# Gate vectors taken as columns, parted weights in two rings, and the pooling sums by a scan

## The chip, the cores and the metric

The kernel runs on one core of a Trainium2 chip. The metric is the device time of one execution in microseconds (us). Engines are named as in the profile: PE is TensorE's matmul side and PEld its weight load, DVE is VectorE, ACT is ScalarE, POOL is GpSimd, SP is SyncE, whose queue (SPq) issues nearly all DMAs here.

## The reference

Two layers of a decoder trunk on 1024 tokens of width 1024, in float32. Each layer has a mixing and a feed-forward sub-layer; both are normalised before and after and modulated by vectors that come from a conditioning vector `c`:

```python
c_act = silu(c)
for l in range(2):
    mod = c_act @ ada_w[l] + ada_b[l]          # 6 vectors of 1024
    shift_m, scale_m, gate_m, shift_f, scale_f, gate_f = split(mod, 6)

    h = rms_norm(x, g_pre_mix[l]) * (1.0 + scale_m) + shift_m
    q, k, v, u = split(h @ w_in[l] + b_in[l], [512, 640, 768])
    q, k = partial_rotary(q), partial_rotary(k)
    attn_out = sliding_window_attention_with_sinks(q, k, v, sinks[l])   # 8 heads of 64, window 128
    pool_out = causal_pool_mixer(u, pool_w[l], pool_scale[l])
    mix = concatenate([attn_out, pool_out]) @ w_out[l]
    x = x + gate_m * rms_norm(mix, g_post_mix[l])

    h = rms_norm(x, g_pre_ffn[l]) * (1.0 + scale_f) + shift_f
    f = (silu(h @ w_gate[l]) * (h @ w_up[l])) @ w_down[l]               # width 2816
    x = x + gate_f * rms_norm(f, g_post_ffn[l])
```

The pooling mixer has four groups of 128 channels. Group g takes, for each token, the mean over the last w = 2, 4, 8 or 16 tokens (fewer at the start), less the token itself, and multiplies by a 128 x 128 matrix.

## The kernel before, in words

**Products.** A float32 product is made of three matmuls of a rounded part `hi` (copied by ACT, L223) and a rest `lo` (subtracted by DVE, L224): hi by hi, hi by lo, lo by hi (`mm3`). Nearly all PE matmuls have 128 x 128 weights and 512 columns. A `STEP` of the hand-written pace is twelve of them. The sequence is handled in two halves of 512 tokens (h = 0, 1) of four tiles of 128.

**Stages of a layer.** First the mixing sub-layer: the projections `u_pass`, `q_pass`, `kv_pass` of a half, with attention and pooling of a half woven between the matmuls, and the output projection `mix_out`. There the order on PE is written out (`manual_schedule`): `weave` takes matmuls of the dense stream and, whenever the count of issued columns has reached a side chain's due time, a step of that chain. A chain's step yields the number of STEPs until it is due again: `LEADS` for the six stages of an attention group (split keys and queries; transposes; first scores; second scores and softmax; probabilities; values), a literal for the pooling mixer, the flow of `ada` weights and the gates. A group is four query heads of one tile of 128 tokens; there are 32 in all. Outside the mixing the order is left to the scheduler, with `run` handing out steps of side streams in proportion to steps of a main stream: first the up projection (`up_pair`, eleven pairs), then the down projection (seven products, 77 steps). In the trace, layer 0's mixing lies at about 75 to 290 us, its up projection until 766, its down projection until about 960; layer 1's mixing at about 970 to 1215, its up projection until 1690, and then its down projection to the end.

**Weights.** `weight` loads 128 x 512 floats into `raw`, then splits them into tiles of the rings `hi` and `lo` (three tiles of 128 x 1024 each, handed out in halves by `part`). Weights that both halves use are written back to DRAM split, and read back for the second half by `weight_once` (L247) as one whole 128 x 1024 tile of the ring `lo`: 28 such loads. `one_ahead` asks for a weight one step before it is used, and in the last `u_pass` two steps. The attention takes halves of `hi` tiles for the split keys and queries.

**Modulation.** A block of 512 values of `mod` is made by DVE: `acc`, 128 x 512, sums eight weight tiles times a column of `c_act` (L368 in the streams, L581 in the flows; eight loads of 256 KB), and PE sums it over the partitions. For scales and shifts of the next layer's mixing `ada_columns` does this with `acc` as weights and a column of ones, four matmuls with one column each, which come out as columns (L512; each float32 matmul appears as two instructions). A gate is a row: `ada_gate` splits `acc` in `hi` and `lo`, multiplies each (L542, L543; 512 columns, one weight column), adds a row of `ada_b`, multiplies a row of the norm's weights and stores the row to DRAM; `load_gate` reads it back onto all partitions. The mixing gate of each layer is made in its own mixing (`gate_flow`), the feed-forward gate in the up projection (`side`), and the next layer's columns in the down projection.

**Pooling.** `pool_mix` makes the sum over w tokens by doubling: log2(w) additions of some 520 elements (L1152), then the mean less the token (L1156), a split, and the matmuls. The tile of `u` has the last 16 tokens of the half before ahead of its 512 tokens (zeros for h = 0).

**End.** In layer 1's last product (`p4`), each evicted block is square-summed by ACT (L614), multiplied by the gate in place (L1778), then scaled and added to the residual in `finish` (from L750), and stored.

## Time and profile before

| | |
|---|---|
| median of three runs | 1868.26 us (1867.52 to 1868.6) |
| profiled execution | 1870.79 us |
| its span | 1869.1 us |
| granted TensorE clock, mean | 0.997 |
| PE busy | 1835.1 us |
| DVE busy | 1501.5 us |
| ACT busy | 919.7 us |
| first PE instruction, last PE end | 11.8 us, 1860.5 us |

The span runs from the first to the last instruction of the profiled execution, whose own time has 1.7 us around it. In lists of waits, a row has the engine and what it made, then what it waited for, then the sum in us, the number of waits and the longest. In a timeline a row has the start, the duration, engine, line, operation, tiles and count, and in brackets the idle time before it with what ended it. In groups a row has the count, the busy us, the mean in ns and the idle time before.

### The profile page before, as it was taken

The numbers are of one execution on the slowest core, as the hardware profiler recorded it, in microseconds if no ns is written. First come the engines' busy times: TensorE is split into PE (matmuls) and PEld (weight loads), VectorE is DVE, ScalarE is ACT, GpSimd is POOL, SyncE is SP. The second block draws the span as 40 slices with busy tenths as digits, with TensorE's granted clock in tenths as the row PEclk, the third lists the DMA queues.
The fourth block names the chain that finished last, engine by engine and source line by source line (L and its number), as shares of the span: only waits on it lengthen the run. The fifth ranks groups of instructions, "written<-read, shape, count | busy, mean of one in ns | idle before, by whom it ended". The sixth has DMA issues, their size and how long they took to land.

```text
span 1869.1 us, 25361 instructions
## 1 busy us (share of the span) xinstructions
PE 1835.1 (98%) x8662; PEld 1515.4 (81%) x8662; DVE 1501.5 (80%) x2492; ACT 919.7 (49%) x1757; POOL 100.3 (5%) x204
## 2 busy tenths in 40 slices
PE   7999999999999999999999999999999999999998
PEld 5888888888888888888887788888887887888886
DVE  7899885688888978879778788856878888877687
ACT  4885785562222223445648559755522222244452
POOL 0021130000000000000001202200000000000000
PEclk9999999999999999999999999999999999999999
DMA  9646744665456556844586676446646456574343
GB/s 341 201 141 215 259 147 143 208 215 181 167 188 218 183 180 225 298 147 133 194 302 202 213 233 217 155 135 209 220 157 207 162 200 229 176 270 142 113 146 114
DMA packets 237089, 363.84 MB, mean 195 GB/s; under 512 B 17912, under 2 KB 126344, under 8 KB 236960
## 3 DMA queue, kind: packets, MB, share of 16 engines
q1 hardware_dynamic: 236352, 360.13, 57.2%
q10 hardware_dynamic: 576, 2.10, 0.3%
q8 instruction: 68, 1.11, 0.2%
q14 instruction: 61, 0.50, 0.1%
q0 software_dynamic: 32, 0.00, 0.0%
HBM read 274.59 MB, written 87.57 MB: 194 GB/s over the span
## 4 chain that ended last, share of the span: by engine, by line
PE 83%; DVE 8%; DMA 4%; ACT 3%; issue 1%; SPq 1%; DVEq 0%; POOL 0%; ACTq 0%; POOLq 0%
PE acc L285 75%; PE msc L285 3%; PE msc L290 2%; PE pv L285 2%; DVE lo L224 1%; DMA raw<-in_w_up_dram 1%; DMA raw<-in_w_in_dram 1%; ACT hi L223 1%; DVE fn L1322 1%; SPq L426 0%; DVE ada L581 0%; DMA ar<-x 0%; DVE st L1026 0%; ACT sb L1034 0%; DVE raw L1337 0%
## 5 line engine op out<-in xcount | busy, mean ns | idle before, releaser
L223 ACT ACTIVATE hi<-raw 128x1024 fp32r<-128x1024 f32 (+2 forms) x360 | 315.6, 889 | 385.2 <-PE acc L285 243.6
L224 DVE TENSOR_TENSOR lo<-raw,hi 128x1024 fp32r<-128x1024 f32 (+2 forms) x360 | 363.0, 1016 | 115.9 <-ACT hi L223 110.7
L285 PE MATMUL acc<-t,hi 128*128 128x512 f32 x1408 | 432.1, 390 | 3.2 <-ACT hi L223 3.2
L285 PEld LDWEIGHTS acc<-t,hi 128*128 128x128 f32 x1408 | 263.6, 188 | 59.7 <-ACT hi L223 5.6
L285 PE MATMUL acc<-t,lo 128*128 128x512 f32 x704 | 271.9, 389 | 0.8 <-DVE lo L224 0.8
L285 PE MATMUL acc<-hT,hi 128*128 128x512 f32 x832 | 260.2, 394 | 0.0
L285 PE MATMUL acc<-hT,lo 128*128 128x512 f32 x608 | 213.4, 393 | 0.5 <-DVE lo L224 0.4
L285 PE MATMUL acc<-bh,hi 128*128 128x512 f32 x520 | 202.8, 390 | 0.0
L285 PE MATMUL acc<-bh,lo 128*128 128x512 f32 x520 | 202.4, 389 | 0.0
L1322 DVE TENSOR_TENSOR fn<-acc,fn 128x512 f32<-128x512 f32 x220 | 150.8, 686 | 33.7 <-PE acc L285 33.6
L285 PEld LDWEIGHTS acc<-hT,hi 128*128 128x128 f32 x832 | 151.8, 188 | 28.1
L285 PEld LDWEIGHTS acc<-t,lo 128*128 128x128 f32 x704 | 132.1, 188 | 30.0 <-DVE lo L224 2.4
L285 PEld LDWEIGHTS acc<-hT,lo 128*128 128x128 f32 x608 | 112.4, 188 | 25.8 <-DVE lo L224 1.3
L285 PE MATMUL acc<-ph,hi 128*128 128x512 f32 x328 | 126.5, 390 | 0.0
L1247 ACT ACTIVATE fn<-fn 128x512 f32<-128x512 f32 x44 | 27.9, 633 | 188.2 <-DVE fn L1322 188.2
L285 PEld LDWEIGHTS acc<-bh,lo 128*128 128x128 f32 x520 | 97.6, 188 | 20.4
L285 PEld LDWEIGHTS acc<-bh,hi 128*128 128x128 f32 x520 | 97.6, 188 | 20.2
L285 PE MATMUL acc<-b,hi 128*128 128x512 f32 x352 | 108.4, 389 | 0.0
L285 PE MATMUL acc<-lo,hT 128*128 128x512 f32 (+1 forms) x352 | 95.8, 349 | 3.9 <-DMA lo<-parted 2.9
L223 ACT ACTIVATE bh<-two_b 128x512 fp32r<-128x512 f32 x100 | 62.3, 623 | 71.2 <-PE acc L285 70.5
L285 PE MATMUL acc<-hi,hT 128*128 128x512 f32 (+1 forms) x320 | 88.8, 351 | 0.6 <-ACT hT L223 0.5
L285 PE MATMUL acc<-hi 128*128 128x512 f32 x224 | 87.6, 391 | 0.8 <-DVE fn L806 0.8
(320 smaller groups left out, 3235.3 us busy)
## 6 DMA issues: line engine op xcount, KB each, us to landing
raw<-in_w_gate_dram SPq DMA_DIRECT2D x44, 512.0 KB
raw<-in_w_up_dram SPq DMA_DIRECT2D x44, 512.0 KB
cfb<-in_ada_w_dram SPq DMA_DIRECT2D x80, 256.0 KB
raw<-keeps SPq DMA_DIRECT2D x40, 512.0 KB
keeps<-fn SPq DMA_DIRECT2D x66, 256.0 KB
ar<-in_ada_w_dram SPq DMA_DIRECT2D x64, 256.0 KB
two_b<-in_w_down_dram SPq DMA_DIRECT2D x30, 512.0 KB
lo<-parted SPq DMA_DIRECT2D x28, 512.0 KB
```

Source lines behind the costliest of these rows:

```text
L223: a = nc.scalar.activation(hi, src, AF.Copy)
L224: v = nc.vector.tensor_sub(lo, src, hi.bitcast(F32))
L285: return nc.tensor.matmul(dst, lhs, rhs, start=start, stop=stop)
L290: return nc.tensor.transpose(dst, src, eye_)
L1247: nc.scalar.activation(g, g, AF.Silu)
L1322: nc.vector.tensor_add(halves_of(dst)[m], bank, halves_of(src)[m])
```

## The change

1. `weight_once` takes the tile for a parted weight from `hi` and `lo` in turn, not always from `lo`.
2. `ada_gate_columns` makes a gate as columns, as `ada_columns` does: four one-column matmuls for a half, the bias and the norm's weights from two more groups of rows in `load_col_rows` (two loads more), and after the second half one transpose, a copy and a store of the row. It is used for both feed-forward gates and for layer 1's mixing gate, which is made in layer 0's down projection; `gate_flow` returns at once in layer 1. Layer 0's mixing gate is made as before.
3. `ada_stream` no longer closes a block at once: the close is appended to `pending`, and `settle`, called at each step of the main stream, carries it out.
4. The scores' scale moves into the copy of the queries; the negative maximum comes from the reduction itself; the sinks are no longer scaled.
5. For w = 8 and 16 `pool_mix` makes the sums by one scan over the tokens, token t in and token t - w out; in the second half it starts from a sum over the w tokens before.
6. In layer 1's last two products the multiplication by the gate writes to a tile of its own (`ready`).
7. Numbers of the pace change: `CLOSE`, `GAPS`, `LEADS`, some gaps, and the down projection's side stream gets 42 steps, not 28.

The diff, cut to its core:

```diff
     def weight_once(key, *srcs):
         if key in parted:
-            both = part("lo", 1024)
+            recent["ring"] = "hi" if recent.get("ring") == "lo" else "lo"
+            both = part(recent["ring"], 1024)
             nc.sync.dma_start(both.bitcast(F32), parted.pop(key))
...
-    NROW = 6 * KD + 2 * KD + 4 + 4
+    NROW = 6 * KD + 4 * KD + 4 + 4
...
-            (pool_scale[l], 4), (b_in[l, QKV:INW], 4),
+            (pool_scale[l], 4), (b_in[l, QKV:INW], 4), (g_post_mix[l], KD), (g_post_ffn[l], KD),
...
+    def ada_gate_columns(l, sub, cols):
+        gates[l, sub] = row = dr.tile([1, D], F32, tag="gate", name="gate", bufs=2 * DEPTH)
+        gc = t_("colp", [P, KD])
+        def close(half, acc):
+            bank = msc_bank()
+            for i in range(4):
+                nc.tensor.matmul(
+                    bank[:, i : i + 1], acc[:, i * P : (i + 1) * P], ones[:, 0:1], start=True, stop=True
+                )
+            o = slice(half * 4, half * 4 + 4)
+            b0 = (3 * sub + 2) * KD
+            g0 = 8 * KD + 8 + sub * KD
+            nc.vector.tensor_add(gc[:, o], bank[:, 0:4], cols[:, b0 + o.start : b0 + o.stop])
+            nc.vector.tensor_mul(gc[:, o], gc[:, o], cols[:, g0 + o.start : g0 + o.stop])
+            if half:
+                pending.append([1, turned])
+        def turned():
+            bank = msc_bank()
+            nc.tensor.transpose(bank[0:KD, :P], gc, ident)
+            rows = t_("ar", [P, 512])[:KD, :P]
+            nc.scalar.activation(rows, bank[0:KD, :P], AF.Copy)
+            nc.sync.dma_start(row.rearrange("o (k p) -> (o k) p", p=P), rows)
...
-    CLOSE = 1.89
-    GAPS = (0.71, 1.06)
+    CLOSE = 1.51
+    GAPS = (0.89, 1.06)
...
+    def settle(steps=1):
+        while due := [p for p in pending if p[0] <= steps]:
+            for p in due:
+                pending.remove(p)
+                p[1](*p[2:])
+            if steps < DONE:
+                break
+        for p in pending:
+            p[0] -= steps
     def ada_stream(jobs):
         for l, n0, close, *whole in jobs:
             got = []
             yield from ada_sum(l, n0, got, *whole)
-            yield from close(*got) or ()
+            pending.append([1, close, *got])
...
-        nc.scalar.activation(qT, bank, AF.Copy)
+        nc.scalar.activation(qT, bank, AF.Copy, scale=SCALE)
...
-        nc.vector.tensor_reduce(mx, S, axis=mybir.AxisListType.X, op=ALU.max)
-        nc.vector.tensor_scalar(mx, mx, -SCALE, None, op0=ALU.mult)
+        nc.vector.tensor_reduce(mx, S, axis=mybir.AxisListType.X, op=ALU.max, negate=True)
...
-    LEADS = (0.9, 0.85, 0.21, 2.72, 1.2, 0.94)
+    LEADS = (0.85, 0.9, 0.25, 2.45, 1.27, 1.0)
...
+            if w >= 8:
+                begin = 0.0
+                if h:
+                    begin = t_("st", [P, 8])[:, 0:1]
+                    nc.vector.tensor_reduce(
+                        begin, u[:, HALO - w : HALO], axis=mybir.AxisListType.X, op=ALU.add
+                    )
+                cur, width = t_("pt", [P, UW])[:, : HALO + T], w
+                nc.vector.tensor_tensor_scan(
+                    cur[:, HALO:n], u[:, HALO:n], u[:, HALO - w : n - w], begin, ALU.add, ALU.subtract
+                )
             while width < w:
...
         def gate_flow():
+            if l:
+                return
...
-            jobs = ada_columns(l + 1, 0, nxt["cols"], nxt["abm"])
-        side = ada_stream(ada_gate(l, 1))
+            jobs = ada_columns(l + 1, 0, nxt["cols"], nxt["abm"]) + ada_gate_columns(l + 1, 0, nxt["cols"])
+        side = ada_stream(ada_gate_columns(l, 1, par["cols"]))
...
-                    nc.vector.tensor_mul(fn[1][t][:, 0:512], fn[1][t][:, 0:512], G[:, 0:512])
-                    finish(1, t, fn[1], ss[1], G, tail[t], aheads[t])
+                    nc.vector.tensor_mul(ready[t][:, 0:512], fn[1][t][:, 0:512], G[:, 0:512])
+                    finish(1, t, ready, ss[1], G, tail[t], aheads[t])
...
-            (between(), 7 * NPAIR), (side, 28),
+            (between(), 7 * NPAIR), (side, 42),
```

More of the change, by code (lines that the diff above doesn't have):

```diff
@@ L551, in ada_gate @@
         ]
+    def ada_gate_columns(l, sub, cols):
[20 more added lines that the diff above has]
+            nc.sync.dma_start(row.rearrange("o (k p) -> (o k) p", p=P), rows)
+        return [
+            (l, (3 * sub + 2) * D + half * 512, lambda acc, half=half: close(half, acc), True)
+            for half in range(2)
+        ]
     def load_gate(l, sub):
@@ L592, in ada_flow @@
         yield from ending
-    CLOSE = 1.89
-    GAPS = (0.71, 1.06)
+    CLOSE = 1.51
+    GAPS = (0.89, 1.06)
     def closing(close, got):
         yield from close(*got) or ()
+    pending = []
+    def settle(steps=1):
[7 more added lines that the diff above has]
+            p[0] -= steps
     def ada_stream(jobs):
@@ L814, in run @@
             i += 1
+            settle()
             for o in others:
@@ L822, in drain @@
             pass
+        settle(DONE)
     halos = {}
@@ L1034, in att_softmax @@
             nc.scalar.activation(
-                S[:, i, :], S[:, i, :], AF.Exp, bias=nm[:, i : i + 1], scale=SCALE, accum_out=sm[:, i : i + 1]
+                S[:, i, :], S[:, i, :], AF.Exp, bias=nm[:, i : i + 1], accum_out=sm[:, i : i + 1]
             )
@@ L1167, in pool_mix @@
             late = (g, hi, lo_)
-            yield 1.7 if h else 2.82
+            yield 1.6 if h else 2.82
         mapped(*late)
@@ L1530, in layer_rows @@
         eng.dma_start(sk, sinks[l : l + 1, :].to_broadcast([P, NH]))
-        nc.vector.tensor_scalar(sk, sk, 1.0 / SCALE, None, op0=ALU.mult)
         d["bq"], d["sink"] = bq, sk
@@ L1642, in gate_flow @@
                 yield 0.5
-            yield from ada_flow([two], [cats[1][1][:, i, :] for i in range(4)], 1.91)
+            yield from ada_flow([two], [cats[1][1][:, i, :] for i in range(4)], 2.49)
         gate = Chain(gate_flow())
@@ L1662, in hybrid_decoder_kernel @@
         ring = [cats[1][1][:, i, :] for i in range(4)]
-        pair = Chain(ada_flow(ada_pair(l, 1, par["cols"], par["abf"]), ring, 0.91))
+        pair = Chain(ada_flow(ada_pair(l, 1, par["cols"], par["abf"]), ring, 0.82))
         weave(out0, late, att, pair)
@@ L1671, in first_half @@
             for _ in post_norm(0, fn, ss, res0):
-                yield 0.59
+                yield 0.55
             while pair.due < DONE:
@@ L1758, in hybrid_decoder_kernel @@
         ss = [t_("ss", [P, 8]) for _ in range(NHALF)]
-        tail, aheads = [], []
+        tail, aheads, ready = [], [], []
         def ended(name, t):
@@ L1768, in ended @@
                 if not nxt:
-                    nc.vector.tensor_mul(fn[1][t][:, 512:D], fn[1][t][:, 512:D], G[:, 512:D])
+                    ready.append(t_("hT", [P, D]))
+                    nc.vector.tensor_mul(ready[t][:, 512:D], fn[1][t][:, 512:D], G[:, 512:D])
                     ahead = t_("st", [P, 8])[:, :1]
```

## The prediction

> **What bounds the kernel now.** I read the busy shares first, then what TensorE (PE) waited for, then the stretches in which it lost time, with their granted clock.
>
> ```profile
> span 1869.1 us, 25361 instructions
> PE 1835.1 (98%) x8662; PEld 1515.4 (81%) x8662; DVE 1501.5 (80%) x2492; ACT 919.7 (49%) x1757; POOL 100.3 (5%) x204
> 325.35 1.36 PE acc L285 x6
> ```
>
> PE is the bound. The third line, from the chain that ended last, gives its pace: six 512-column matmuls in 1.36 us, 0.227 us each. Work removed elsewhere pays only where PE waits for it. The table of waits, PE's own:
>
> ```profile
> PE msc L402 <- DVE ident L156: 11.8, 1, 11.8
> PE acc L285 <- ACT hi L223: 3.2, 4, 1.4
> PE acc L285 <- DMA lo<-parted: 2.9, 2, 1.6
> PE msc L285 <- ACT qT L999: 2.5, 3, 0.9
> PE acc L285 <- DVE lo L224: 2.2, 4, 1.0
> ```
>
> Beside the start (11.8 us) there are some 11 us of waits in four kinds. The second, two waits for a load of a parted weight, costs more than its 2.9 us. The busy times by stretch (us; PE, PEld, DVE, ACT, POOL, then granted clock and DMA share) show it:
>
> ```profile
> 1020.00:1034.00 14.00, 13.73 (x77) 11.10 (x76) 13.33 (x29) 11.00 (x30) 3.12 (x7) 1.00 0.62 200
> 1041.00:1043.00 2.00, 0.77 (x3) 0.48 (x3) 2.00 (x5) 1.65 (x8) 1.15 (x1) 1.00 0.57 179
> 1043.00:1045.00 2.00, 0.43 (x2) 0.22 (x2) 1.97 (x8) 0.70 (x3) 0.00 (x0) 0.78 0.84 300
> 1045.00:1047.00 2.00, 2.00 (x5) 1.62 (x6) 1.10 (x2) 0.63 (x1) 0.00 (x0) 0.50 0.84 248
> 1047.00:1050.00 3.00, 3.00 (x14) 2.43 (x13) 0.16 (x1) 1.57 (x3) 0.00 (x0) 0.50 0.11 40
> 1050.00:1051.00 1.00, 1.00 (x4) 0.81 (x3) 0.00 (x0) 0.87 (x2) 0.00 (x0) 0.52 0.40 45
> ```
>
> In layer 1's mixing PE idles 2.8 us between 1041 and 1045 (4.00 less 0.77 and 0.43), and then runs at half clock for six microseconds, which costs half of them: 3.0 us. Together 5.8 us, the largest loss after the start. [...]
>
> **The late load.** SyncE's queue (SP) before the stall, and the two waits:
>
> ```profile
> 1026.16 4.77 SPq L568 DMA_DIRECT2D cfb<-in_ada_w_dram  x5
> 1032.19 2.41 SPq L568 DMA_DIRECT2D cfb<-in_ada_w_dram  x3
> 1034.98 0.85 SPq L236 DMA_DIRECT2D raw<-in_w_out_dram  x2
> 1037.26 0.34 SPq L247 DMA_DIRECT2D lo<-parted  x1
> 1040.94 0.34 SPq L247 DMA_DIRECT2D lo<-parted  x1
> 1042.23 0.98 PE L285 MATMUL acc<-lo,hT 128*128 128x512 f32 x3 [1.32 <-DMA lo<-parted]
> 1044.78 1.65 PE L285 MATMUL acc<-lo,hT 128*128 128x512 f32 x3 [1.57 <-DMA lo<-parted]
> SPq L247 <- PE acc L285: 41.8, 17, 7.6
> ```
>
> The load of 1037.26 lands 5.0 us later, the next is issued only at 1040.94. Two causes: every parted weight takes one of three `lo` tiles, and L247 waits 41.8 us in all until matmuls free one (last line, SP's own waits); and eight gate-weight loads, 256 KB each, go through the same queue and engines in those ten microseconds.
>
> **The change, part by part.** *Parted weights alternate between `hi` and `lo`*: a slot comes free twice as early, from two rings of three. *Layer 1's mixing gate leaves this stage*: its 16 ada loads (4 MB) move into layer 0's down projection. Either one moves the load ahead. What is late next is the attention's own work, which had over a microsecond to spare there, since PE was stalled. I take 5.4 of 5.8 us as gained (**-5.4**), with bounds 0 (the wait remains) and 5.8.
>
> *PE work of the gates.* A half's close was two 512-column matmuls (L542, L543); it becomes four pairs of one-column passes, as L512 does them now:
>
> ```profile
> 765.37 0.94 PE L512 MATMUL msc<-ones_r,ada 128*128 128x1 f32 x8
> 766.18 0.49 PE L285 MATMUL acc<-bh,hi 128*128 128x512 f32 x1
> 1436.30 0.40 PE L542 MATMUL msc<-ph,picks 128*1 128x512 f32 x1
> 1436.77 0.43 PE L285 MATMUL acc<-t,lo 128*128 128x512 f32 x1
> ```
>
> From start to the next start: 0.81 us (766.18 less 765.37) against 0.47 us (1436.77 less 1436.30): +0.34 us for each of six halves (three gates), 2.0 us. Each gate adds a transpose in two passes; bounded by 0 and the 0.47 us of two wide matmuls, I take 0.2: 0.6 in all. On PE, all of it on the path: **+2.6 us**. For each gate one copy on ACT and one store of the row replace six small loads and stores; the row is read back a stage later, which hides them. The `pending` list delays a close by a step of the main stream, in which PE has its matmuls; without that cover it costs the 0.8 us of a close. Scaling in the query copy and without the sinks' scaling adds no instruction.
>
> *VectorE (DVE).*
>
> ```profile
> L1027 DVE TENSOR_SCALAR st<-st 128x4 f32<-128x4 f32 x32 | 6.1, 191 | 0.2
> L1152 DVE TENSOR_TENSOR pt<-pt 128x525 f32<-128x525 f32 (+2 forms) x24 | 19.0, 790 | 0.4
> L1152 DVE TENSOR_TENSOR pt<-uT 128x527 f32<-128x527 f32 x16 | 11.2, 700 | 1.7 <-ACT uT L918 1.7
> L1412 DVE TENSOR_TENSOR two_b<-two_b,hT 128x1024 f32<-128x1024 f32 x20 | 24.1, 1225 | 3.4 <-DMA two_b<-in_w_down_dram 3.3
> L212 DVE RECIPROCAL rcnt<-rcnt 128x64 f32<-128x64 f32 x1 | 0.5, 544 | 0.0
> 980.00:1070.00 90.00, 12.63 (x17) 0.96 0.65 204
> ```
>
> The negation folded into the maximum removes 32 instructions of 0.19 us, 6.1 us, one from each softmax chain. Of the 40 doubling additions 28 go (3 and 4 in each of four mixes): 8 x 0.70 + 20 x 0.79 = 21.4 us. Eight scans come, and four short sums at about 0.19 us. No row shows a scan. Below it costs what an addition costs (0.70); above, at the reciprocal's rate past its first 0.16 us, (0.544 - 0.16)/64 x 512 + 0.16 = 3.2 us. Add and subtract of one token must be done before the next begins, so I charge two element times: the row for 1024 elements, 1.22 us. Then 21.4 - 9.8 - 0.8 = 10.8 us leave DVE (bounds 15.0 and -5.0). [...] The last line (the L581 group alone) is the moved gate: 12.6 us of accumulation out of a stretch whose DVE is 95% busy (13.33 of 14.00 above). DVE is late for PE only in part of these stages: of the waits for `lo` from DVE (2.2 us) I take half as gained, **-1.0**, with bounds 0 and 2.2.
>
> *Leads.* Transposed queries get 0.05 step more before their scores; a step is twelve matmuls, 2.72 us, so 0.14 us for each of the three waits on qT: **-0.4**. The softmax lead falls by 0.27 step, 0.73 us, against 0.19 us from the removed negation; a few of the 32 groups will now be late by some tenths: **+0.3**, bounds 0 and 32 x 0.54 = 17.
>
> *Down projection of layer 0.* It takes 16 more loads and accumulations. Its DVE:
>
> ```profile
> 800.00:850.00 50.00, 50.00 (x230) 41.62 (x229) 37.11 (x51) 20.97 (x32) 0.00 (x0) 1.00 0.44 142
> 850.00:900.00 50.00, 50.00 (x226) 41.49 (x226) 48.05 (x75) 31.04 (x53) 0.00 (x0) 1.00 0.48 162
> ```
>
> The 12.6 us are spread over 55 of its 77 steps (six blocks of five steps, at 42 for 77). Where DVE has 13 us free they hide; in 850 to 900 it has 2, and about 4 come. The buffers ahead of PE cover the rest but for **+0.5**; bounds 0 and 12.6. DMA at about half share hides the 4 MB.
>
> *Up projection.* The gate's split and wide row operations leave ACT and DVE; two of the four waits on `hi` stand just before such a close (PE L542 at 1436.30 follows one). The accumulations that delay the weights stay: **-0.3** of 3.2 us.
>
> *The tail.* The last product's evicted block is multiplied in place, so it waits for ACT's square sum:
>
> ```profile
> 1861.92 0.63 ACT L614 ACTIVATE junk<-sb 128x512 bf16<-128x512 f32 x1 [2.92 <-DVE sb L1417]
> 1862.67 0.69 DVE L1778 TENSOR_TENSOR sb<-sb,G 128x512 f32<-128x512 f32 x1 [0.85 <-ACT junk L614]
> 1863.28 0.15 DVE L750 SCALAR_TENSOR_TENSOR rs<-ss,st 128x1 f32<-128x1 f32 x1
> ```
>
> Into another tile it runs beside the square sum, and L750 follows the sum at about 1862.7: **-0.6**.
>
> *The start.* Two more small loads go ahead of the first ada weights on SP, which is on the chain there:
>
> ```profile
> 2.78 0.29 SPq L396 DMA_DIRECT2D ar<-in_b_in_dram  x1
> ```
>
> Two at 0.29 us: bounds 0 and 0.6, I take **+0.3**.
>
> **Sum.** -5.4 + 2.6 - 1.0 - 0.4 + 0.3 + 0.5 - 0.3 - 0.6 + 0.3 = -4.0 us. The profiled execution took 1870.8 us (1.7 around its span), 2.5 above the median of 1868.26. From the median: **1864.3 us**. If all of these 2.5 us belong to the stall, it is smaller without the profiler, and the time 1866.8; if the smaller waits go too (2.1 more of qT, 1.2 of `lo`, 1.3 of `hi`), 1859.7.
>
> **Rivals.** *The load stays late.* One weight is still asked for only one step ahead, and the output weights' loads still stand before it in SP's queue (1034.98 above). For it: that order is not changed. Against it: half the slots' pressure and 4 MB are gone. Then 5.4 us are not gained: 1869.7, no change.
>
> *Slower: the `hi` ring.* Attention's keys and queries are split into `hi` tiles; half of the 28 parted loads now sit in that ring until their matmuls are done. Where a split has to wait for such a tile, the group comes a k-step of twelve matmuls late, 2.7 us. Two such delays eat the gain, and from the third on (3 x 2.72 = 8.2, less 4.0, over 3.7) the kernel is slower. At five of fourteen it takes 1864.3 + 13.6 = 1877.9. For it: PE waited on qT already in three places. Against it: a split holds its half tile only until its transposes.
>
> *Faster still: DVE's relief.* Over 20 us leave DVE in layer 1's mixing; if the short waits above go and the down projection hides everything, 1864.3 less 4.6 and 0.5: 1859.2.
>
> **How the numbers follow.** Forecast 0.59, load late 0.14, `hi` ring 0.16, relief 0.11. A measurement of this kernel tells about 0.2% (3.7 us) from no change, so the line lies at 1864.5 and the forecast just beyond it; its own range is 1860 to 1867. I give 0.42 of its 0.59 to faster, since PE's waits of 11 us and the half clock leave more to gain than the sum takes, and 0.17 to the same. Faster is 0.42 + 0.11 = 0.53, same 0.17 + 0.14 = 0.31, slower the ring's 0.16. The range 1857.5 to 1872.5 leaves out some 0.1 above (a ring with four delays or more) and 0.1 below.
>
> **What would show it.** No PE wait on a parted weight near 1040 and a granted clock of 1.00 there; scan rows near 1.2 us; L512-like closes at 0.8 us; L1778's successor without its wait on ACT; no new waits of PE between 850 and 910. Wrong would be: PE waits on qT or `hi` grown beyond 5 us, half clock in another stretch, or DVE at 100% over 30 us of layer 0's down projection with PE waiting behind it.

## The result, and the profile after

The changed kernel takes a median of 1873.22 us (1870.77 to 1875.8) against 1868.38 us (1867.5 to 1871.01) before: a ratio of 1.0026, interval [1.0017, 1.0035]. It is slower by a little more than the 0.2% that can be told from no change, where 1864.3 us was predicted, and 0.7 us above the predicted range. Its profiled execution took 1873.18 us.

The head of the page after:

```profile
span 1871.5 us, 25338 instructions
PE 1835.5 (98%) x8701; PEld 1518.5 (81%) x8701; DVE 1479.7 (79%) x2436; ACT 915.9 (49%) x1754; POOL 92.5 (5%) x204
```

DVE lost 21.8 us of work (1501.5 less 1479.7) and the kernel is not faster: PE is as busy as before. PE's waits, in the kernel after, without the start's (engine and product, what it waited for, us in all, times, longest):

```profile
PE acc L286 <- ACT hi L223: 4.6, 4, 2.5
PE msc L291 <- ACT sa L1025: 3.5, 2, 2.2
PE msc L291 <- DVE hi L1033: 1.6, 2, 0.8
PE msc L291 <- DVE pth L224: 1.1, 2, 0.8
PE acc L286 <- DVE qkv L935: 0.9, 1, 0.9
PE acc L286 <- DVE fn L1473: 0.9, 2, 0.6
PE acc L286 <- DVE sb L1473: 0.7, 1, 0.7
```

The waits on a parted weight, on `qT` and on `lo` are gone from the list; the prediction had the first wholly and the others in part. In their place stand waits of transposes (L291) in the mixing, for ACT's copy of the turned keys (L1025, tile `sa`) and for the split queries (L1033, tile `hi`), and of the down projection on its own evictions (L1473, and L935 in the projection after it). Busy times of the kernel after, by stretch (PE, PEld, DVE, ACT, POOL, granted clock, DMA share):

```profile
1020.00:1034.00 14.00, 14.00 (x79) 11.73 (x78) 10.62 (x24) 10.83 (x33) 2.94 (x6) 1.00 0.31 98
1034.00:1052.00 18.00, 17.26 (x91) 14.32 (x90) 12.32 (x27) 14.56 (x44) 5.01 (x11) 1.00 0.78 234
766.00:800.00 34.00, 33.40 (x150) 27.44 (x151) 30.18 (x46) 16.20 (x28) 0.00 (x0) 1.00 0.88 312
800.00:850.00 50.00, 50.00 (x230) 41.62 (x229) 45.03 (x60) 21.26 (x32) 0.00 (x0) 1.00 0.57 183
850.00:900.00 50.00, 49.01 (x223) 40.10 (x222) 46.06 (x73) 27.51 (x42) 0.00 (x0) 1.00 0.51 162
200.00:305.00 105.00, 101.95 (x531) 84.57 (x530) 79.13 (x162) 82.83 (x203) 21.88 (x40) 1.00 0.52 181
1120.00:1240.00 120.00, 117.88 (x604) 97.89 (x603) 88.76 (x177) 93.00 (x228) 21.84 (x40) 1.00 0.53 180
```

The same stretches of the two second halves in the kernel before:

```profile
200.00:305.00 105.00, 104.65 (x544) 87.03 (x543) 83.71 (x174) 83.89 (x207) 22.30 (x40) 1.00 0.54 189
1120.00:1240.00 120.00, 119.88 (x612) 99.42 (x611) 90.75 (x186) 93.47 (x227) 23.07 (x40) 1.00 0.53 178
```

In layer 1's first half (1020 to 1052) PE now idles 0.74 us at full clock. In the second halves it idles 3.05 us of 105 (before 0.35) and 2.12 us of 120 (before 0.12); in layer 0's down projection 0.60 and 0.99 us, where before had nothing.

To see where time went in every kernel I took from each trace the start of the same accumulating matmul (of the 7272 matmuls into `acc`, by count) at ten places, and compared it with a second profiled execution of the kernel before (span 1866.4 us, below). The steps, in us, a positive one is time lost in that stage; they are worked out from the traces, are no rows of them, and hold for one execution each. "First" and "second" are the halves of a mixing; the crossing runs from the down projection into layer 1.

| kernel | 1st, layer 0 | 2nd, layer 0 | up 0 | down 0 and crossing | 1st, layer 1 | 2nd, layer 1 | up 1 | tail | all |
|---|---|---|---|---|---|---|---|---|---|
| before (first profile) | -0.6 | 0.1 | -1.2 | -0.1 | 3.0 | 0.4 | 1.4 | 0.0 | 2.7 |
| after | -3.2 | 3.4 | 3.7 | 6.1 | -6.6 | 2.1 | 0.7 | -1.3 | 5.1 |
| after, again | -3.3 | 2.4 | 1.6 | 5.2 | -6.0 | 2.1 | 1.4 | -1.3 | 1.8 |
| rings alone | -1.1 | 1.3 | 1.5 | -0.1 | -3.3 | 1.7 | -0.2 | 0.0 | 0.1 |
| scan alone | -0.2 | 3.2 | -0.7 | 0.0 | 2.7 | 2.3 | 0.1 | 0.0 | 7.6 |
| moved gate alone | -0.3 | 0.0 | 0.5 | 4.7 | -0.7 | 0.4 | -0.5 | -0.2 | 3.1 |
| moved gate and rings | -0.4 | 1.4 | 2.3 | 5.2 | -6.6 | 1.7 | -1.0 | -0.2 | 1.7 |
| after, rows for all gates | -3.3 | 3.3 | 1.6 | -0.4 | -4.3 | 2.0 | 3.5 | -1.2 | 0.5 |
| after, parted only in `lo` | -3.3 | 1.6 | 4.3 | 5.1 | -0.9 | 1.1 | 1.6 | -1.3 | 7.6 |
| after, old pace numbers | -0.2 | 2.8 | 3.3 | 5.1 | -6.5 | 3.2 | 0.6 | -1.3 | 6.5 |
| first halves only | -2.7 | 0.9 | 1.2 | 0.2 | -3.8 | 0.6 | -0.8 | -1.2 | -5.2 |

(The start and the second down projection, each within 0.7 us, are left out of the columns, not of the sum.) The up projections scatter by -1 to 4 us even where nothing in them was changed, so a single column there proves little; the others repeat to about a microsecond in the two profiles of the changed kernel.

### The profile page after: what moved, and what is told of

The parts are those of the page before. It is cut to its first block, busy times and chain, and to the rows that moved or that the text cites. A ratio compares the mean times of both kernels' runs of the same rounds, so it can differ in the third digit from the quotient of the medians.

```text
span 1871.5 us, 25338 instructions
## 1 busy us (share of the span) xinstructions
PE 1835.5 (98%) x8701; PEld 1518.5 (81%) x8701; DVE 1479.7 (79%) x2436; ACT 915.9 (49%) x1754; POOL 92.5 (5%) x204
## 4 chain that ended last, share of the span: by engine, by line
PE 79%; DVE 9%; DMA 6%; ACT 4%; issue 2%; SPq 0%; DVEq 0%; POOL 0%; ACTq 0%; POOLq 0%
PE acc L286 70%; PE msc L286 3%; PE msc L291 2%; PE pv L286 2%; DVE lo L224 1%; DMA ar<-in_ada_w_dram 1%; DMA ar<-x 1%; ACT hi L223 1%; DMA raw<-in_w_gate_dram 1%; DMA raw<-in_w_up_dram 1%; ACT sb L1079 1%; DVE fn L1378 1%; DMA raw<-in_w_in_dram 1%; DVE ada L369 0%; ACT raw L711 0%
## 5 line engine op out<-in xcount | busy, mean ns | idle before, releaser
L286 PE MATMUL acc<-hT,hi 128*128 128x512 f32 x928 | 288.3, 396 | 0.0
L286 PEld LDWEIGHTS acc<-hT,hi 128*128 128x128 f32 x928 | 168.2, 188 | 30.6
L286 PE MATMUL acc<-hT,lo 128*128 128x512 f32 x512 | 188.5, 392 | 0.1
L286 PEld LDWEIGHTS acc<-hT,lo 128*128 128x128 f32 x512 | 95.4, 188 | 20.7 <-DVE fn L850 0.9
L286 PE MATMUL acc<-hi,hT 128*128 128x512 f32 (+1 forms) x416 | 108.1, 349 | 1.7 <-DVE qkv L935 0.9
L286 PE MATMUL acc<-lo,hi 128*128 128x512 f32 x224 | 87.3, 390 | 0.0
```

The lines of the kernel that those rows point to most:

```text
L286: return nc.tensor.matmul(dst, lhs, rhs, start=start, stop=stop)
```

## Theories

*A, the moved gate:* what the change wins in layer 1's first half it pays back in layer 0's down projection, where the gate's 16 loads and accumulations now go. *B, the second halves:* their hand-written order fits the old durations and tiles; the alternating rings, the scan and the new pace numbers shift it, and PE waits. *Rivals:* that the one-column closes or the `pending` list cost more than counted; that the new pace numbers are the loss; that the scan is slow.

## The experiments

The expectations letter their theories each for itself; the letters there are not always the two above.

**The two kernels again**, for a second profile of each.

> The kernel before, profiled once more. If the stall at 1041 to 1051 us (two waits on parted weights, then half clock) belongs to the kernel, the trace shows it again, with a granted clock near 0.8 between 1034 and 1052, and a time of 1868 us or more. If it was an accident of that one execution, the waits on parted weights are gone and the execution takes 4 to 6 us less than the first profiled one, about 1865.

> The changed kernel, profiled once more. What belongs to the schedule shows again: PE waits of about 3.5 us on ACT sa (near 220 and 1144 us) and 1.6 us on DVE's split queries, closes of 0.8 us in layer 0's down projection. What was an accident goes: the wait of 2.5 us on hi at 624 us and its half clock.

Times 1868.08 and 1869.92 us. The before's second profile, PE's waits and the stretch of the stall:

```profile
PE acc L285 <- DMA lo<-parted: 2.6, 2, 1.6
1034.00:1052.00 18.00, 15.44 (x83) 12.41 (x82) 14.44 (x33) 12.40 (x37) 3.90 (x9) 1.00 0.80 260
```

Both waits are there as in the first profile, but the granted clock stays at 1.00. So the half clock, 3.0 of the 5.8 us that the prediction counted as the stall, does not come in every execution. Eight profiled executions here have their parted weights in `lo` alone and the wait for them: over 1040 to 1062 the granted clock is 0.84 in the first profile of the kernel before, 0.92 in five (scan alone, gates alone, each close at once, moved gate alone, the changed kernel without rings) and 1.00 in two (this one, the moved gate again). 0.92 over 22 us is 1.8 us lost, half of what the first profile lost (3.5). After's loss in the down projection and in the second halves is there again.

**Rings alone**, on the kernel before:

```diff
+            recent["ring"] = "hi" if recent.get("ring") == "lo" else "lo"
+            both = part(recent["ring"], 1024)
```

> The kernel before with one edit: parted weights take tiles of hi and lo in turn. Theory A (the change lost its time to the moved and column-wise gate work, not to the rings): the wait for a parted weight near 1040 us and the half clock behind it go, 5 to 6 us less, 1862 to 1864 us. Theory B (parted tiles in the hi ring hold up attention's splits, the slower rival of the prediction): PE waits on splits of queries or keys appear, 1870 us or more. If the late load came from the gate's loads alone, the stall stays: 1867 to 1869.

1868.07 us, ratio 1.0000 [0.9988, 1.0013]. The rings alone take the parted waits away (they are in none of its rows of waits of PE) and win 3.3 us there; they lose 1.3 and 1.7 us in the two second halves. No gain is left.

**The changed kernel with the rings taken back** (parted weights only in `lo`):

```diff
-            recent["ring"] = "hi" if recent.get("ring") == "lo" else "lo"
-            both = part(recent["ring"], 1024)
+            both = part("lo", 1024)
```

> The changed kernel with all parted weights in lo again. If the rings bring what the prediction took (5.4 us), 1877 or more. If they are worth nothing in most executions, as rings_alone has it, within 1 us of 1873.2, a ratio near 1.0026. If hi tiles taken by parted weights hold up attention's splits (ACT's wait of 5.0 us on PE before the key split), 1870 or less.

1875.67 us, ratio 1.0044 [1.0027, 1.006]. One row of PE's waits of it:

```profile
PE acc L285 <- DMA lo<-parted: 3.8, 1, 3.8
```

The gate is out of this stage here, and the load is still late: the rings are what makes it early, not the relief of the queue. Its second halves lose 1.6 and 1.1 us against 3.4 and 2.1 (2.4 and 2.1 in the second profile): some two fifths to a half of that loss is the rings'.

**All gates as rows in their old places**, the rest of the change kept:

```diff
-            if l:
-                return
-            jobs = ada_columns(...) + ada_gate_columns(l + 1, 0, nxt["cols"])
-        side = ada_stream(ada_gate_columns(l, 1, par["cols"]))
-            (between(), 7 * NPAIR), (side, 42),
+            jobs = ada_columns(...)
+        side = ada_stream(ada_gate(l, 1))
+            (between(), 7 * NPAIR), (side, 28),
```

> The changed kernel with all gates as rows and layer 1's mixing gate back in its mixing: rings, scan, folded scale, own tile at the end and new paces stay. Theory A (column gates on PE and the moved work are the cost): both single steps gave some 0.07% against the changed kernel's 0.26%, together 0.14% or more, a ratio to the kernel before of 1.0012 or less, 1868 to 1870.5 us. If the two steps overlap, 1.0019 again.

1869.85 us, 1.0008 [0.9999, 1.0016]. The down projection's loss is gone (-0.4 us).

**Only layer 1's mixing gate back** in its own mixing, the feed-forward gates still columns:

```diff
         def gate_flow():
-            if l:
-                return
-            jobs = ada_columns(...) + ada_gate_columns(l + 1, 0, nxt["cols"])
-            (between(), 7 * NPAIR), (side, 42),
+            jobs = ada_columns(...)
+            (between(), 7 * NPAIR), (side, 28),
```

> The changed kernel, but layer 1's mixing gate is made in layer 1's mixing again, as a row; the down projection's side stream has 28 steps again. Theory A: layer 0's down projection is some 5 us faster (no closes of 0.8 us each, none of the four waits on evictions by DVE), and the mixing of layer 1 gives back up to 3 us of DVE's relief: 1867 to 1871, faster than the changed kernel's 1873.2. Theory C (the new paces order the mixing badly, and the gate's place matters little): 1872 to 1874.

1871.9 us, 1.0019 [1.0008, 1.003]. **Only the feed-forward gates as rows:**

```diff
-        side = ada_stream(ada_gate_columns(l, 1, par["cols"]))
+        side = ada_stream(ada_gate(l, 1))
```

> The changed kernel, but both feed-forward gates are made as rows again (a split and two wide matmuls for a half). Theory A with PE work alone: two gates at 0.9 us, 1.8 us less, 1871.4. If the column closes also shift the up projection's weights (PE waits 2.7 us on hi at 624 us and runs at half clock for 3 us): up to 5 us less, 1868. Theory C: within 1 us of 1873.2.

1871.09 us, 1.0019 [1.0006, 1.0032]. Both lie between the whole change and the kernel with all gates as rows, with overlapping intervals; these two do not tell the gates apart. The next do.

**The gates alone**, on the kernel before (`ada_gate_columns`, its two groups of rows, `pending`, 42 steps; no rings, scan, folding or pace numbers), then **only layer 1's mixing gate moved** (the same, with the line of the feed-forward gates left as `ada_gate(l, 1)`), then **the gates alone with each close at once**:

```diff
-            pending.append([1, close, *got])
+            close(*got)
-                pending.append([1, turned])
+                turned()
```

> The kernel before with only the gates changed: columns, the pending list, layer 1's mixing gate moved into layer 0's down projection with 42 steps; parted weights in lo, old paces, no scan. Theory A (the gates are the cost, the other parts gain): PE gets 2.6 us more work, layer 0's down projection and what follows it lose about 5.3 us, the mixing of layer 1 gains 2 to 3 us: 3 to 5 us more than before, a ratio of 1.0015 to 1.003. If the gates are neutral, 1.000.

> The kernel before with layer 1's mixing gate alone moved into layer 0's down projection, as columns (42 steps, pending list); the feed-forward gates stay rows, nothing else changes. Theory D (the moved gate carries most of the gates' 10 us): layer 0's down projection and what follows it +5.5 to 6 us, layer 1's first half of the mixing -0.5, since the parted weights still wait: a ratio of 1.002 to 1.003. Theory E (the feed-forward gates' column closes carry it): 1.001 or less.

> The kernel before with all the gates' changes, but each close at once and not by the pending list. If the delay makes PE wait (the accumulator's one buffer is free only a step later), layer 0's down projection falls from +5.3 to about +3, PE's own work: a ratio of 1.004 or less, against 1.0053 with the list. If only the work counts: 1.0053.

1877.69 us, 1.0053 [1.0041, 1.0065]; 1877.87 us, 1.0056 [1.0043, 1.0068]; 1878.5 us, 1.0062 [1.0043, 1.0081]. The moved gate is the whole loss of the gates; the feed-forward columns add nothing to it that these runs can tell (the three intervals overlap), and the `pending` list is not its cause. In the moved gate's own profile, DVE's waits between 741 and 960 us, then PE's between 741 and 980:

```profile
DVE ada L368 <- DMA ar<-in_ada_w_dram: 8.8, 10, 1.7
```

```profile
PE acc L285 <- DVE sb L1462: 0.7, 1, 0.7
PE acc L285 <- DVE qkv L934: 0.6, 1, 0.6
```

**The moved gate profiled again**, and **the moved gate with the rings** (the diff of the rings above on top of it):

> moved_only profiled once more: its profiled execution was the fastest of its six, 6.7 us below their median. If the usual execution loses more in the same places, layer 0's down projection or the parted weights' waits (with half clock) are larger here, and the execution takes 1875 us or more; else about 1871.

> The kernel before with the moved gate (columns) and the rings together. If the moved gate's large loss (1.0056) is in the waits on parted weights, which still stand in layer 1's first half without the rings, the rings take most of it away: 1.000 to 1.002, with the gate's stage still +5 us. If it is in the down projection alone: 1.005.

1872.57 us; and 1872.63 us, 1.0028 [1.0016, 1.004]. The parted wait of the moved gate alone (2.7 us in both its profiles) is gone with the rings. In layer 1's stall, first the moved gate alone, then with the rings:

```profile
1034.00:1052.00 18.00, 15.27 (x72) 12.08 (x72) 13.54 (x33) 10.89 (x36) 4.71 (x10) 0.94 0.76 236
```

```profile
1034.00:1052.00 18.00, 18.00 (x101) 15.37 (x100) 11.79 (x29) 13.70 (x43) 5.19 (x11) 1.00 0.69 222
```

About half of the moved gate's loss goes with the rings. One thing stays open: its two profiled executions (1871.15 and 1872.57 us) are faster than all its others (1875.21 to 1880.46 us), so some 5 us of its usual loss stand in no trace of this kernel. The nearest is the trace of the gates alone (1877.96 us, a usual execution): by the same count it loses 6.2 us in the down projection and its crossing, 1.2 and 2.9 us in the up projections, and 9.9 in all.

**The scan alone** on the kernel before, and **the changed kernel without the scan**:

```diff
+            if w >= 8:
+                begin = 0.0
+                if h:
+                    ...
+                cur, width = t_("pt", [P, UW])[:, : HALO + T], w
+                nc.vector.tensor_tensor_scan(
+                    cur[:, HALO:n], u[:, HALO:n], u[:, HALO - w : n - w], begin, ALU.add, ALU.subtract
+                )
```

> The kernel before with one edit: the sums over 8 and 16 tokens by the scan. The prediction's step: 10.8 us leave DVE, of which at most 2 us reach PE; 1866 to 1868.5, a ratio of 0.999 to 1.000. Rival (a scan of 1.2 to 1.4 us holds DVE while attention's splits wait, and costs the second halves of the mixing 1 to 2 us each): a ratio of 1.001 or more.

> The changed kernel with the doubling additions again. If the scan helps as predicted, up to 2 us more: a ratio to the kernel before of 1.003 to 1.004. If the scan costs the second halves of the mixing, these lose their 2 to 3.4 us against the kernel before and the ratio falls to 1.0015 or less.

1874.2 us, 1.0036 [1.0022, 1.0049]; and 1875.35 us, 1.0045 [1.0033, 1.0057]. Put into the old order, the scan makes it slower, though it takes work from DVE: 3.2 and 2.3 us in the second halves. Taken out of the new order, it does not make that faster either (the median is higher, the intervals touch). Second halves without the scan lose as much (3.8 and 2.7 us, by the same count). The scan's own duration is not the loss.

**The old pace numbers** in the changed kernel (`CLOSE`, `GAPS`, `LEADS` and the gaps as before):

```diff
-    LEADS = (0.85, 0.9, 0.25, 2.45, 1.27, 1.0)
+    LEADS = (0.9, 0.85, 0.21, 2.72, 1.2, 0.94)
...
```

> The changed kernel with all numbers of the pace (CLOSE, GAPS, LEADS, gaps of the flows, the pooling's yield) as before. Theory A: within 1.5 us of 1873.2, the new waits of the mixing on ACT near 220 and 1144 us change their place only. Theory C: these waits and those on the split queries near 254 and 1177 us go, some 6 us of PE's time: 1867 to 1869.

1874.89 us, 1.0044 [1.0027, 1.0061]. That rival falls: with the new numbers layer 0's first half is 3 us shorter (-3.2 against -0.2), and the loss of the second halves is much the same in sum (2.8 and 3.2 us with the old ones), though made of other waits, as told below.

**Rows for all gates, and the rings without the parted weights of `u`:**

```diff
-            recent["ring"] = "hi" if recent.get("ring") == "lo" else "lo"
+            recent["ring"] = "hi" if recent.get("ring") == "lo" and key[0] != "u" else "lo"
```

> Scan, folded scale, own tile at the end and new paces, all gates as rows in their old places, and the rings in turn only for the parted weights of queries, keys and values; those of the pooling inputs stay in lo. Read from the stages: first halves of the mixing -3.2 and -4.3 us, the second halves +1.7 and +0.8 without the hi ring's part, the end -1.2, the rest 0: about 6 us less than the kernel before, a ratio of 0.997. If the ring of the pooling weights is not what costs the second halves, 1.0008 as with all rings.

1868.19 us, 1.0000 [0.999, 1.0011]. Its second halves lose 1.6 and 1.3 us, where with rings for all they lost 3.3 and 2.0. Without the moved gate, the gate columns and `u` in the rings, the change costs nothing and brings nothing; some 0.3% less had been expected.

**First halves only.** On the kernel before, what won there: rings without `u`, the multiplication into an own tile at the end, and the new `LEADS` and the one gap in the first halves; the second halves keep the old numbers. Then the same, with the folded scale and negation, and the scan in the first halves:

```diff
+    LEADS_OF = ((0.85, 0.9, 0.25, 2.45, 1.27, 1.0), (0.9, 0.85, 0.21, 2.72, 1.2, 0.94))
-            yield from ada_flow([two], [cats[1][1][:, i, :] for i in range(4)], 1.91)
+            yield from ada_flow([two], [cats[1][1][:, i, :] for i in range(4)], 2.49)
```

```diff
+            if w >= 8 and not h:
+                ...
+                nc.vector.tensor_tensor_scan(...)
-        nc.scalar.activation(qT, bank, AF.Copy)
+        nc.scalar.activation(qT, bank, AF.Copy, scale=SCALE)
...
```

> The kernel before with three parts of the change: the tile of its own at the end, rings in turn for the parted weights of queries, keys and values, and the new leads and gate gap in the first halves of the mixing only. By the stages of the runs so far: first half of layer 0 -2.4 us, of layer 1 -3.5, second halves 0 to +0.7 each, end -1.2: 6 to 7 us less, a ratio of 0.9965. If the second halves lose whatever is changed ahead of them, 0.999 to 1.000.

> As first_half_paces, with the scan in the first halves only and the folded scale and negation in both. The first halves gain 0.8 us more; if the folded scale leaves the second halves alone, a ratio of 0.996; if it shifts their order, +1.5 us in each and 0.998.

1866.7 us, 0.9993 [0.9982, 1.0005], less of a gain than expected; and 1863.35 us, **0.9972 [0.9962, 0.9981]**, faster than both kernels. Of the second, PE's waits, then its second halves:

```profile
PE acc L286 <- ACT hi L223: 4.3, 3, 1.7
PE msc L291 <- DVE pth L224: 1.6, 2, 0.8
PE msc L286 <- ACT qT L1000: 1.1, 1, 1.1
```

```profile
200.00:305.00 105.00, 104.50 (x542) 86.72 (x541) 82.16 (x165) 83.36 (x204) 22.26 (x40) 1.00 0.54 183
1120.00:1240.00 120.00, 119.54 (x609) 99.52 (x608) 86.15 (x170) 90.33 (x215) 22.17 (x40) 1.00 0.51 170
```

PE idles 0.50 and 0.46 us in the second halves against 3.05 and 2.12, while the first halves keep 2.7 and 3.8 us of their gain. This kernel leaves out the moved gate (A) and keeps the second halves' own numbers (B); since it leaves out both at once, with the gate columns, it does not price them apart. Two steps on the way there stand clear of each other's intervals: all gates as rows (1.0026 to 1.0008), and the second halves mostly as they were (1.0000 to 0.9972).

## Why the prediction was wrong, step by step

*The late load (-5.4): right in place, too large in size.* PE waits on no parted weight any more, and the clock is 1.00 there. The mechanism needs the rings (moved gate alone: a wait of 2.7 us left; without rings: 3.8 us). But the sum took its size from one execution in which the two waits had also halved the clock for longer than in any other trace, and set it against a median of executions that need not have that. Without the half clock some 2.6 us of wait were there to gain; with it, as most of the eight traces have it, 1.8 more. The text named this case (1866.8 us) and did not choose it. Layer 1's first half did gain 6.6 and 6.0 us against the second profile, because the closes (0.9 us) and waits on `qT` (2.2 us there) went too.

*Layer 0's down projection (+0.5): the step that failed.* It measures 6.1 and 5.2 us. Counted by the starts of the matmuls around them, two closes and a transpose of the moved gate are 2.1 us of the 6.1, which the prediction had under PE work. Most of the rest is waits: three on evictions (L1473: 0.60, 0.72 and 0.27 us, 2.4 us with the slower start behind each, whose first matmul takes 0.50 us where those before the wait take 0.39) and one of 0.9 us on `qkv` (L935) in the crossing. The words "The buffers ahead of PE cover the rest" are where it went wrong. DVE's time in 850 to 900 is below what I feared (46.06 of 50). What I did not see is its order. After, DVE's waits between 741 and 960 us; before, the same row has 0.6 us in one wait, in the second profile 1.0 us in three:

```profile
DVE ada L369 <- DMA ar<-in_ada_w_dram: 10.2, 10, 1.9
```

And one of these ten in the timeline after:

```profile
790.10 1.13 SPq L377 DMA_DIRECT2D ar<-in_ada_w_dram  x2
796.32 0.75 DVE L369 SCALAR_TENSOR_TENSOR ada<-ar,c_act,ada 128x512 f32<-128x512 f32 x1 [1.86 <-DMA ar<-in_ada_w_dram]
796.99 0.68 DVE L1473 TENSOR_TENSOR fn<-acc,sb 128x512 f32<-128x512 f32 x1
797.73 0.50 PE L286 MATMUL acc<-bh,hi 128*128 128x512 f32 x1 [0.60 <-DVE fn L1473]
```

One of the two loads issued from 790.10 on lands at 796.3, with DMA at 0.88 of its share over 766 to 800. DVE stands at the accumulation that needs it, 1.86 us, and the eviction behind it in the same queue starts only at 796.99; PE waits 0.60 us for that eviction. An average of DVE's free time hides this: the accumulation was priced by its duration and not by the wait that it brings into the queue. Ahead of the wait of 0.72 us DVE had stood 1.45 and 0.31 us for such loads; ahead of the one of 0.27 no accumulation stands. Ahead of the one on `qkv` DVE had stood 2.34 us for a load of the residual (L770), the same pattern with another load. That the gate brings these waits is shown by the runs without it (-0.4 us); how it does is read from the order of the rows, and no run held the loads back or moved them alone. The prediction's own sign, no new waits of PE between 850 and 910, failed with the 0.72 and the 0.27 us.

*The second halves (-0.4 on `qT`, +0.3 for the softmax lead): the other step that failed.* `qT` did as said. But the new waits of 3.5 and 1.6 us in the list above, all four of them in the second halves, were in no term. The slower rival had the place right (the split queries in `hi`) for the 1.6 us, and neither its price nor its point: no group was late by a k-step of 2.7 us, the waits are 0.8 to 2.2 us. The wait on the split queries is there in every trace that has both the rings for `u` and the scan, and in none that lacks one of them. Around the largest, after:

```profile
212.62 1.38 SPq L248 DMA_DIRECT2D hi<-parted  x1
214.09 0.39 SPq L761 DMA_DIRECT2D x<-fn  x1
220.44 1.15 ACT L700 ACTIVATE fn<-fn,rs 128x1024 f32<-128x1024 f32 x1 [0.81 <-DMA x<-fn]
221.50 0.58 ACT L1022 ACTIVATE sa<-msc 128x512 fp32r<-128x512 f32 x1
221.97 0.59 ACT L1025 ACTIVATE sa<-msc 128x512 fp32r<-128x512 f32 x1
222.61 0.66 PE L291 MATMUL msc<-ident,fn 128*128 128x128 f32 x4 [2.23 <-ACT sa L1025]
```

What waits is the transposes of a residual block (`fn`), until ACT has copied the turned keys out of a bank (L1025). Ahead of that copy ACT's queue has two normalisations of residual blocks (L700). Here a store of the block goes out behind a parted load in SP's queue, and the second normalisation waits 0.81 us for it; the two copies behind it in ACT's queue start at 221.50 and 221.97. But that explains only what this wait has above 1.3 us: in layer 1, and in both layers of the second profile, the same transposes wait 1.3 us with no such store ahead. The other traces say more. Before, the same two normalisations stand ahead of the same copy and PE does not wait; with rings alone the wait is 0.3 us, with everything but the new pace numbers 0.3, with everything but the rings 0.9, with both 1.3 and more. So most of this wait comes with the new pace numbers, and more of it with the rings. The old numbers do not win it back in sum, since other waits (0.9, 0.6, 0.5 and 0.5 us in each second half) stand there in its place. Why the copy comes late against PE in one order and not in the other stays open.

*The gates' PE work (+2.6): right.* A close measures 0.80 us from start to next start, the transpose 0.27 us (L575, one matmul a gate, where the prediction had two passes); six closes at 0.80 less 0.47 and three transposes are 2.8 us.

```profile
541.08 0.95 PE L562 MATMUL msc<-ones_r,ada 128*128 128x1 f32 x8
541.88 0.72 PE L286 MATMUL acc<-t,hi 128*128 128x512 f32 x2
```

*The scan (1.22 us): right in its duration, and no gain by itself (1.0036 when put in alone).* The two forms of L1202 after (ns: smallest, median, largest), without and with a starting sum:

```profile
L1202 DVE TENSOR_TENSOR_SCAN pt<-uT x4: 1211/1214/1219, 110.6 to 1036.1; 128x512 f32<-128x512 f32 x4
L1202 DVE TENSOR_TENSOR_SCAN pt<-uT,st x4: 1273/1375/1481, 254.5 to 1180.2; 128x512 f32<-128x512 f32 x4
```

The prediction's 1.22 us was an estimate, two element times for a token, taken from the plain row for 1024 elements (L1412, 1225 ns); the scan of 512 measures 1.21 us without a starting sum. What sets its length is shown by no row. The -1.0 for DVE's relief is not seen as such: two of the waits for `lo` did go, and others came.

*The tail (-0.6): right in its mechanism, and half of what came (-1.3).* The stretch from the last eviction to the last scaling was 1861.14 to 1864.49 (3.35 us; L1778 and L750 in the prediction's rows lie in it) and is now:

```profile
1864.23 0.69 DVE L1473 TENSOR_TENSOR sb<-acc,sb 128x512 f32<-128x512 f32 x1
1865.77 0.16 DVE L794 SCALAR_TENSOR_TENSOR rs<-ss,st 128x1 f32<-128x1 f32 x1
1866.98 1.42 DVE L816 SCALAR_TENSOR_TENSOR hT<-hT,rs 128x512 f32<-128x512 f32 x2
```

That is 2.75 us, 0.60 less. As much again came ahead of the eviction. In the timeline before, DVE still had the scaling of the block before it when PE was done (1860.5):

```profile
1859.81 1.42 DVE L772 SCALAR_TENSOR_TENSOR sb<-sb,rs,hT 128x512 f32<-128x512 f32 x2
1861.14 0.68 DVE L1417 TENSOR_TENSOR sb<-acc,sb 128x512 f32<-128x512 f32 x1
1864.49 1.41 DVE L772 SCALAR_TENSOR_TENSOR sb<-sb,rs,hT 128x512 f32<-128x512 f32 x2
```

Now the shorter chain of that block is over in time, and the eviction starts 0.04 us after the last matmul's end (1863.80 and 0.39), not 0.64. The prediction took the one block and not the one ahead of it.

*The start (+0.3)* stayed within 0.1 us. *The up projection (-0.3)* can't be told: it moved by -1 to 4 us without cause in the code.

*Not foreseen: layer 0's first half.* It gains 3.2 us. Gone there are waits of 1.6 us on `lo` and 0.7 on `qT` (second profile of before), for which the prediction had -1.0 and -0.4 in all. That the new pace numbers would bring it was not foreseen: with the old ones the gain is 0.2 us. They are not enough alone: in the kernel with the new leads in the first halves, without scan and folding, it is 1.1 us by the same count.

By the table, then, 11.1 us were gained (3.2, 6.6, 1.3), and three places that had been priced at 0.4 us together, beside the closes, took 11.6 (6.1, 3.4, 2.1). Of the 4.4 us in the up projections, the rest of the 5.1, 1.7 are the half clock behind a wait of 2.55 us (last section), which the second profile of the changed kernel does not have; there they are 3.0. What is left of them has no cause shown.

## What to carry to other kernels

Price a moved accumulation by what stands behind it in its engine's queue while its load is late, not by the free share of that engine. Where the order is written by hand, a saving is first a shift: bring it in where the trace shows PE waiting (here the first halves), and leave the stretches without waits as they are until they are paced anew. And take the size of a stall from two executions at least, above all if a lowered clock is part of it.

## What the runs showed of the hardware

The clock falls after some short waits and not after others of nearly the same size. In the prediction's rows waits of 1.32 and 1.57 us, with about 1 us of work between them, gave 0.50; in the second profile of the kernel before these two left it at 1.00:

```profile
1043.75 0.96 PE L285 MATMUL acc<-lo,hT 128*128 128x512 f32 x3 [0.98 <-DMA lo<-parted]
1046.29 0.98 PE L285 MATMUL acc<-lo,hT 128*128 128x512 f32 x3 [1.57 <-DMA lo<-parted]
```

In the changed kernel one wait of 2.55 us was enough, in an up projection (its matmuls, then the stretch):

```profile
626.60 1.77 PE L286 MATMUL acc<-t,hi 128*128 128x512 f32 x4 [2.55 <-ACT hi L223]
```

```profile
624.00:630.00 6.00, 3.45 (x10) 2.68 (x10) 6.00 (x8) 2.95 (x3) 0.00 (x0) 0.75 0.39 135
```

Its four matmuls take 1.77 us, where six took 1.36 in the prediction's row of the pace. The clock records of this case's 20 traces show where it fell. From the start to 1840 us the clock is halved 14 times in all, 13 times for 3.41 us and once, in the first profile of the kernel before, for 6.83; and the time at full clock between two changes is always a whole number of 3.413 us (1027.4 us in the first profile of the kernel before, 611.0 and 1239.0 in the first of the changed kernel, are 301, 179 and 363 of them). So within each of these traces the changes lie on a grid of 3.41 us. Cut into windows along it, by the profile's busy times (the ends of matmuls are modelled), each of the 11 windows at full clock in which PE is busy less than 0.45 of the time is followed by half clock, 3 of the 14 between 0.45 and 0.51 are, and of the 10657 above, none. These counts are worked out from the traces, are no rows of them, and hold for these traces alone. The windows of the stall, in the first and then in the second profile of the kernel before:

```profile
1040.72:1044.13 3.41, 1.17 (x4) 0.48 (x3) 3.41 (x7) 1.99 (x10) 1.15 (x1) 1.00 0.71 247
1044.13:1047.54 3.41, 2.76 (x7) 2.10 (x8) 2.10 (x6) 0.99 (x3) 0.00 (x0) 0.50 0.79 245
```

```profile
1040.81:1044.22 3.41, 2.43 (x11) 1.72 (x10) 3.41 (x7) 1.18 (x7) 2.77 (x4) 1.00 0.78 234
1044.22:1047.64 3.42, 1.84 (x9) 1.17 (x8) 3.39 (x9) 1.86 (x7) 0.00 (x0) 1.00 0.88 300
```

PE is busy 1.17 of 3.41 us in the first (0.34), and 2.43 and 1.84 in the others (0.71 and 0.54): nearly the same waits, falling otherwise on the grid. In the changed kernel the window of the wait of 2.55 us, 623.55 to 626.97, has PE busy for 0.87 of 3.42 us (0.25), and the next 3.41 us have a granted clock of 0.50: PE was not idle for a whole window. In these traces a fall of the clock costs half of 3.41 us, 1.7 us, and 3.4 in the first profile of the kernel before: the size of the differences asked about here.
